# V rows of one token tile gathered token by token and summed on TensorE, and all gate matrices built before the last front

## The chip, the core and the metric

The kernel is one program on one core of a Trainium2 chip. The metric is the device time of one execution in microseconds. The core has TensorE (PE), VectorE (DVE), ScalarE (ACT), GpSimd (POOL) and SyncE (SP), each with its own queue of instructions that it takes in order, and 16 DMA engines that all queues share. TensorE runs at one of two clocks, 1.2 or 2.4 GHz; the profile gives the granted clock as a share of the higher one.

## The reference, cut to what matters

A sequence of 1024 tokens with 1024 features runs through one layer: a mixer (three recurrent branches, HGRN2, S5 and RG-LRU, between two projections) and a PEER layer with 16384 experts. Each expert is one row of `u_tab` and one row of `v_tab`. For each token, eight heads pick 16 experts each, so a token has 128 slots.

```python
x = x + gt1 * (y @ w_out[l])
h2 = rms_norm(x, g_ffn[l]) * (1.0 + sc2) + sh2
...
act = jax.nn.gelu(jnp.einsum('td,thkd->thk', hb, u_tab[eb]))
out = jnp.einsum('thk,thkd->td', gb * act, v_tab[eb])
x = x + gt2 * out          # then a final rms_norm
```

Everything is fp32.

## The kernel before

The 1024 tokens are eight tiles of 128. They go through the mixer in four fronts of two tiles each, F0 to F3; a front ends with the product keys (`product_keys`), which choose the experts of its two tiles. The recurrences make F0 to F3 follow one another.

The PEER layer is worked in two ways. Tiles 0, 1, 6 and 7 are gathered. In the U phase of a tile, slot k gathers for each of the 128 tokens the row of its k-th expert from `u_tab` (an indirect DMA on GpSimd's queue, 128 rows of 4 KB, into a buffer `row`), and VectorE multiplies it with the token's features and sums (L929). The V phase gathers from `v_tab`, again tokens on partitions, and VectorE adds weight times row to `fin` (L944). There are four buffers `row` in the fronts and a fifth in the dense stage.

Tiles 2 to 5 (`DSET`) are dense: every expert is computed for all of their 512 tokens, and the result is weighted with a gate matrix that is zero where a token did not choose the expert. `gates` builds these matrices: for each quad of four tokens it makes one-hot rows of the two halves of the expert number (`oh`), multiplies them on TensorE (`gk`), copies to `stg`, and stores 16 tokens at a time to `gd` in DRAM. There are 32 quads in a tile. `dense` then streams both tables through TensorE: transposes, products A with the features, gelu, the gates, products V.

The order is set in two steps. `PLAN` lists the steps: `("F", b)` is a front, `("P", u, v)` gathers the U slots of tile u and the V slots of tile v, `("G", n)` builds n gate matrices, `("D",)` is the dense stage, `("R",)` adds the fifth row buffer, `("E",)` ends. From that a planner with its own cost model arranges each engine's queue ahead of time by priority. Steps P carry a handicap of `PRI` = 3000 places, so they fill gaps. Work that comes later in the list may start earlier when its inputs and a free buffer are there. `dense` closes the pools of the fronts and puts its own tiles in their place, so it starts only when the fronts, their routing and all gate matrices are done; the row buffers stay.

The list before reads: F0, P(0, -), F1, F2, two gate matrices, P(-, 0), P(1, -), F3, two gate matrices, dense, R, P(-, 1), P(6, -), P(7, 6), P(-, 7), E.

Of the kernel before, what the change touches and what calls it, by code (L numbers as in the profile page):

```python
# [10 lines left out]
F32 = mybir.dt.float32  # L11
I32 = mybir.dt.int32
# [28 lines left out]
RTG = ()  # L41
RTS = ()
OHB = 1
GPRI = [0, 0, 0, 0]
SCP = 3
RSB = 2
PRI = 3000
# [16 lines left out]
PAD = 320  # L64
HRN = 2
EB = 3
PLAN = [("F", 0), ("P", 0, None), ("F", 1), ("F", 2), ("G", 2), ("P", None, 0), ("P", 1, None), ("F", 3), ("G", 2), ("D",), ("R",), ("P", None, 1), ("P", 6, None), ("P", 7, 6), ("P", None, 7), ("E",)]
NH = 4
HP = 8
TOPK = 16  # L70
# [17 lines left out]
def trunk(ctx, tc, x, c, w_mod, b_mod, g_mix, w_in, hgrn_lb_logits, s5_a_re, s5_a_im, s5_b_re, s5_b_im,  # L88
# [56 lines left out]
    V.memset(ones, 1.0)  # L145
    epsc = keep.tile([128, 1], F32, name="epsc")
    V.memset(epsc, EPS)
    one = keep.tile([128, 1], F32, name="one")
    V.memset(one, 1.0)

    iof = keep.tile([128, 128], F32, name="iof")
    G.iota(iof, [[1, 128]], base=0, channel_multiplier=0, allow_small_or_imprecise_dtypes=True)
# [194 lines left out]
    def front(t0, NT):  # L347
# [27 lines left out]
        def s5_parts():  # L375
# [23 lines left out]
            V.tensor_tensor(w[:, :, :, 0], w[:, :, :, 0], x_[:, :, :, 0], OP.add)  # L399
            yield  # L400
            for ri in range(2):
                if n == dec.shape[-1]:
                    wf = w[:, ri].rearrange("p k n -> p (k n)")
                    V.tensor_tensor_scan(wf, dec.rearrange("p k n -> p (k n)"), wf, 0.0, OP.mult, OP.add)
                else:
                    for k in range(8):
                        V.tensor_tensor_scan(w[:, ri, k], dec[:, k, 0:n], w[:, ri, k], 0.0, OP.mult, OP.add)

            xs = T4().rearrange("p (r k n) -> p r k n", r=2, k=8)[:, :, :, 0:n]
            V.tensor_copy(xs[:, :, :, 0], s5s)  # L410
# [329 lines left out]
    def route(r, eid, j):  # L740
        dense = j is not None
        best, ef = r
        if dense:
            sc4 = sm.tile([128, 2 * 8 * NCAND], F32, name="oh", bufs=OHB)
            tf = sc4[:, 0:2 * NS].rearrange("p (a s) -> p a s", a=2)
            ti = sc4[:, 2 * NS:4 * NS].bitcast(I32).rearrange("p (a s) -> p a s", a=2)
            eid = sc4[:, 4 * NS:5 * NS].bitcast(I32)
            V.tensor_copy(eid, ef.rearrange("p h k -> p (h k)"))
            gate = sc4[:, 5 * NS:6 * NS].rearrange("p (h k) -> p h k", h=HP)
        else:  # L750
            gate = pk_.tile([128, HP, TOPK], F32, name="gate", bufs=EB)
        V.tensor_tensor(gate, best, best[:, :, 0:1].to_broadcast([128, HP, TOPK]), OP.subtract)
        S.activation(gate, gate, AF.Exp)
        gs = sm.tile([128, HP], F32, name="gs")
        V.tensor_reduce(gs, gate, AX.X, OP.add)
        V.reciprocal(gs, gs)
        V.tensor_tensor(gate, gate, gs.unsqueeze(2).to_broadcast([128, HP, TOPK]), OP.mult)
        if not dense:
            return eid, gate

        V.tensor_single_scalar(ti[:, 0], eid, 7, OP.arith_shift_right)
        V.tensor_single_scalar(ti[:, 1], eid, 127, OP.bitwise_and)
        V.tensor_copy(tf, ti)
        bk = ph.tile([128, 512], F32, name="rt").rearrange("p (a s) -> p a s", a=4)
        P_.transpose(bk[:, 0], tf[:, 0], ident)
        P_.transpose(bk[:, 1], tf[:, 1], ident)
        P_.transpose(bk[:, 2], gate.rearrange("p h k -> p (h k)"), ident)
        tT = gp.tile([128, 3, NS], F32, name="tT", bufs=len(DSET))
        S.copy(tT, bk[:, 0:3])
        return tT, None  # L770
# [13 lines left out]
    def gates(j, tT):  # L784

        for c in range(128 // GT):
            stg = gp.tile([128, NK, GT], F32, name="stg", bufs=1)
            for q in range(GT // 4):
                pg = pg_.tile([128, 4, 128], F32, name="gk")
                oh = gp.tile([128, 2, 4, 128], F32, name="oh2", bufs=OB)  # L790

                for i in range(4):
                    t = c * GT + q * 4 + i
                    V.tensor_scalar(oh[:, 0, i], iof, tT[:, 0, t:t + 1], tT[:, 2, t:t + 1], op0=OP.is_equal, op1=OP.mult)
                    S.activation(oh[:, 1, i], iof, AF.Abs, bias=tT[:, 1, t:t + 1], scale=-1.0)
                S.activation(oh[:, 1], oh[:, 1], AF.Relu, bias=one, scale=-1.0)  # L796
                for i in range(4):
                    mm(pg[:, i], oh[:, 1, i], oh[:, 0, i], True, True)
                S.copy(stg[:, :, q * 4:q * 4 + 4].rearrange("p a t -> p t a"), pg)  # L799
            D.dma_start(out=gd[j * (128 // GT) + c], in_=stg)  # L800
# [136 lines left out]
    def v_slot(o, k):  # L937
# [5 lines left out]
        else:  # L943
            V.scalar_tensor_tensor(o.fin, vr, o.wgt[:, k:k + 1], o.fin, op0=OP.mult, op1=OP.add)  # L944

    def v_end(o):
        t, tmp = o.t, o.fin
        V.tensor_tensor(tmp, tmp, bcast["gt2"], OP.mult)
        finish(t, tmp, row)
# [46 lines left out]
    def slots(tu, tv):  # L996
# [11 lines left out]
        if v is not None:  # L1008
            v_end(v)

    head = front(*blocks[0])
    ahead = [head]
    next(head)
# [218 lines left out]
    for k in range(8):  # L1232
        V.scalar_tensor_tensor(toep[:, k], ident, dcol[:, k:k + 1], toep[:, k], op0=OP.mult, op1=OP.add)


    NST = TBM // T4S
    dec = const.tile([128, 8, NST], F32, name="dec")
    V.tensor_copy(dec, mT.unsqueeze(2).to_broadcast([128, 8, NST]))
    V.memset(dec[:, :, 0:1], 0.0)
    tau = CS()[:, 0:NST]  # L1240
    G.iota(tau, [[1, NST]], base=1, channel_multiplier=0, allow_small_or_imprecise_dtypes=True)
    rotc = const.tile([128, 8, NST], F32, name="rotc")
# [24 lines left out]
    for step in PLAN:  # L1267
# [9 lines left out]
        elif step[0] == "D":  # L1277
            dense()
        elif step[0] == "R":
            rows_.extend(more)  # L1280
        elif step[0] == "E":
            dense_end()
        else:
            phase(step[1], step[2])
# [31 lines left out]
```

## Time and profile before

| | us |
|---|---|
| median of 3 runs | 3267.55 (3264.48 to 3271.3) |
| the profiled execution | 3274.55 |
| its span, first to last instruction | 3272.8 |

| engine | busy, us | share of the span |
|---|---|---|
| PE (matmul) | 2853.3 | 87% |
| DVE | 2654.4 | 81% |
| POOL | 1305.0 | 40% |
| ACT | 1121.9 | 34% |

Busy time is the union of an engine's instructions. Matmuls are pipelined, so the mean duration of one is longer than its share of the busy time. An fp32 matmul leaves two records. A wait is put down to the instruction that released it.

### The profile page before, as it was taken

The numbers are of one execution on the slowest core, as the hardware profiler recorded it, in microseconds if no ns is written. First come the engines' busy times: TensorE is split into PE (matmuls) and PEld (weight loads), VectorE is DVE, ScalarE is ACT, GpSimd is POOL, SyncE is SP. The second block draws the span as 40 slices with busy tenths as digits, with TensorE's granted clock in tenths as the row PEclk, the third lists the DMA queues.
The fourth block names the chain that finished last, engine by engine and source line by source line (L and its number), as shares of the span: only waits on it lengthen the run. The fifth ranks groups of instructions, "written<-read, shape, count | busy, mean of one in ns | idle before, by whom it ended". The sixth has DMA issues, their size and how long they took to land.

```text
span 3272.8 us, 46195 instructions
## 1 busy us (share of the span) xinstructions
PE 2853.3 (87%) x16525; PEld 2439.7 (75%) x16525; DVE 2654.4 (81%) x5925; ACT 1121.9 (34%) x2123; POOL 1305.0 (40%) x1155
## 2 busy tenths in 40 slices
PE   5998975788778985678679999999999999999997
PEld 3765855476676865557569888988988988988886
DVE  6241898689987999768869889988999999899845
ACT  3212321123387651575822222222222222222222
POOL 0000146534444346430235545555555555455301
PEclk8998986899679985778589999999999999999998
DMA  5353687999689986894399989999999999899822
GB/s 153 115 155 122 183 293 242 324 340 303 210 286 350 310 283 222 285 325 140 134 319 338 326 307 336 348 345 345 338 344 349 343 352 347 311 330 341 297 91 78
DMA packets 490373, 896.77 MB, mean 274 GB/s; under 512 B 29608, under 2 KB 306720, under 8 KB 486048
## 3 DMA queue, kind: packets, MB, share of 16 engines
q0 software_dynamic: 147456, 536.94, 46.1%
q1 hardware_dynamic: 333312, 342.92, 32.0%
q10 hardware_dynamic: 9376, 13.96, 1.3%
q8 instruction: 131, 2.15, 0.3%
q14 instruction: 98, 0.80, 0.1%
HBM read 847.57 MB, written 46.14 MB: 273 GB/s over the span
## 4 chain that ended last, share of the span: by engine, by line
PE 41%; DVE 20%; DMA 16%; issue 11%; ACT 6%; POOL 5%; ACTq 0%; SPq 0%; POOLq 0%; DVEq 0%
PE A L139 13%; PE V L139 12%; PE bank L139 8%; DMA row<-in_peer_u_dram,eid 5%; DVE row L929 4%; PE wq L139 4%; POOL row L923 4%; DVE fin L944 3%; DMA row<-in_peer_v_dram,eid 3%; PE gk L139 2%; PE T L844 2%; DMA gd<-stg 2%; ACT stg L799 1%; POOL row L939 1%; DMA vn<-in_peer_v_dram 1%
## 5 line engine op out<-in xcount | busy, mean ns | idle before, releaser
L939 POOL DMA_INDIRECT row<-in_peer_v_dram,eid x512 | 622.2, 1215 | 691.2 <-DVE fin L944 360.4
L923 POOL DMA_INDIRECT row<-in_peer_u_dram,eid x512 | 638.2, 1246 | 622.9 <-DVE row L929 282.1
L139 PE MATMUL V<-vh,w 128*128 128x256 f32 x4096 | 768.6, 283 | 11.3 <-ACT vh L869 4.7
L929 DVE SCALAR_TENSOR_TENSOR row<-row,h 128x1024 f32<-128x1024 f32 x512 | 619.1, 1219 | 95.6 <-DMA row<-in_peer_u_dram,eid 92.0
L944 DVE SCALAR_TENSOR_TENSOR fin<-row,wgt,fin 128x1024 f32<-128x1024 f32 x508 | 649.4, 1278 | 50.0 <-DMA row<-in_peer_v_dram,eid 45.0
L139 PEld LDWEIGHTS V<-vh,w 128*128 128x128 f32 x4096 | 644.8, 189 | 22.2 <-ACT w L858 5.4
L139 PE MATMUL V<-vl,w 128*128 128x256 f32 x2048 | 562.1, 281 | 8.5 <-DVE vl L871 8.4
L139 PE MATMUL A<-hh,ul 128*128 128x512 f32 x1024 | 408.9, 399 | 14.6 <-DVE ul L846 14.6
L139 PE MATMUL A<-hh,uh 128*128 128x512 f32 x1024 | 416.6, 407 | 0.4 <-ACT uh L845 0.3
L139 PE MATMUL A<-hl,uh 128*128 128x512 f32 x1024 | 404.7, 395 | 0.0
L139 PEld LDWEIGHTS V<-vl,w 128*128 128x128 f32 x2048 | 389.0, 190 | 14.0 <-DVE vl L871 10.4
L869 ACT CAST vh<-vn 128x1024 fp32r<-128x1024 f32 x128 | 134.7, 1052 | 457.0 <-PE V L139 385.0
L139 PE MATMUL bank<-hT,w 128*128 128x256 f32 x1152 | 271.5, 392 | 20.8 <-DMA w<-in_w_in_dram 11.6
L139 PE MATMUL gk<-oh 128*128 128x128 f32 x1024 | 195.5, 352 | 95.8 <-ACT oh L796 56.3
L139 PEld LDWEIGHTS gk<-oh 128*128 128x128 f32 x1024 | 176.8, 255 | 117.9 <-ACT oh L796 81.4
L139 PEld LDWEIGHTS bank<-hT,w 128*128 128x128 f32 x1152 | 221.4, 197 | 56.6 <-issue 10.9
L139 PE MATMUL wq<-hT,w 128*128 128x256 f32 x1024 | 238.9, 388 | 5.1 <-DMA w<-in_peer_w_q_dram 5.1
L845 ACT CAST uh<-T 128x512 fp32r<-128x512 f32 x256 | 147.4, 586 | 273.7 <-PE T L844 267.9
L139 PEld LDWEIGHTS A<-hh,ul 128*128 128x128 f32 x1024 | 195.1, 191 | 54.8 <-DVE ul L846 21.1
L139 PEld LDWEIGHTS A<-hl,uh 128*128 128x128 f32 x1024 | 194.7, 190 | 37.1
L139 PEld LDWEIGHTS A<-hh,uh 128*128 128x128 f32 x1024 | 195.1, 190 | 34.8 <-ACT uh L845 1.3
L139 PEld LDWEIGHTS wq<-hT,w 128*128 128x128 f32 x1024 | 194.9, 195 | 31.2 <-issue 5.2
(422 smaller groups left out, 4084.6 us busy)
## 6 DMA issues: line engine op xcount, KB each, us to landing
vn<-in_peer_v_dram SPq DMA_DIRECT2D x128, 512.0 KB
un<-in_peer_u_dram SPq DMA_DIRECT2D x128, 512.0 KB
w<-in_w_in_dram SPq DMA_DIRECT2D x88, 512.0 KB
w<-in_peer_w_q_dram SPq DMA_DIRECT2D x64, 512.0 KB
gd<-stg SPq DMA_DIRECT2D x32, 1024.0 KB
gt<-gd SPq DMA_DIRECT2D x16, 2048.0 KB
w<-in_w_mod_dram SPq DMA_DIRECT2D x48, 512.0 KB
w<-in_w_out_dram SPq DMA_DIRECT2D x32, 512.0 KB
```

The lines of the kernel that those rows point to most:

```text
L139: P_.matmul(o, l, r, start=st, stop=sp)
L799: S.copy(stg[:, :, q * 4:q * 4 + 4].rearrange("p a t -> p t a"), pg)
L844: P_.transpose(bk[:, k], un[:, kk * 128:kk * 128 + 128], ident)
L845: S.copy(uh, bk)
L869: S.copy(vh, vn)
L923: G.indirect_dma_start(out=ur, out_offset=None, in_=u_tab, in_offset=bass.IndirectOffsetOnAxis(ap=o.eid[:, k:k + 1], axis=0))
L929: V.scalar_tensor_tensor(ur, ur, 1.0, o.h2, op0=OP.mult, op1=OP.mult, accum_out=o.act[:, k:k + 1])
L939: G.indirect_dma_start(out=vr, out_offset=None, in_=v_tab, in_offset=bass.IndirectOffsetOnAxis(ap=o.eid[:, k:k + 1], axis=0))
L944: V.scalar_tensor_tensor(o.fin, vr, o.wgt[:, k:k + 1], o.fin, op0=OP.mult, op1=OP.add)
```

## The change

The V phase of tile 0 is done by a new step M (`v_matmul`). It transposes expert numbers and weights of the tile, so that the 128 slots of a token lie on partitions. For each half of the 1024 features and each i from 0 to 31 it gathers the half rows (2 KB each) of the experts of four tokens, i, 32 + i, 64 + i and 96 + i: four gathers into two `row` buffers. Each token's 128 half rows are then multiplied by its weights on TensorE. The stationary operand is a slice of 32 columns of `zq`, zero but for one column that ScalarE fills with the weights of that token, and the result adds into one of four strips of 32 partitions of a PSUM bank. After 32 steps VectorE multiplies the bank by `gt2`.

Further parts: all four gate matrices stand ahead of F3 in the list, the last two with a handicap of 500 and 900 places (`GPRI`); in `gates` VectorE makes both one-hots with one comparison and ScalarE scales one of them by the gate, in place of Abs and Relu; the transposes of the gate rows move from the bank `rt` to `gk`, and M's sum takes that bank; the S5 scan runs over 64 elements at a time and its table `dec` goes.

```diff
-GPRI = [0, 0, 0, 0]
+GPRI = [0, 0, 500, 900]
...
-PLAN = [("F", 0), ("P", 0, None), ("F", 1), ("F", 2), ("G", 2), ("P", None, 0), ("P", 1, None), ("F", 3), ("G", 2), ("D",), ("R",), ("P", None, 1), ("P", 6, None), ("P", 7, 6), ("P", None, 7), ("E",)]
+PLAN = [("F", 0), ("P", 0, None), ("F", 1), ("F", 2), ("G", 4), ("M", 0), ("P", 1, None), ("F", 3), ("D",), ("R",), ("P", None, 1), ("P", 6, None), ("P", 7, 6), ("P", None, 7), ("E",)]
...
             for ri in range(2):
-                if n == dec.shape[-1]:
-                    wf = w[:, ri].rearrange("p k n -> p (k n)")
-                    V.tensor_tensor_scan(wf, dec.rearrange("p k n -> p (k n)"), wf, 0.0, OP.mult, OP.add)
...
+                for k in range(8):
+                    V.tensor_tensor_scan(w[:, ri, k], mT[:, k:k + 1].to_broadcast([128, n]), w[:, ri, k], 0.0,
+                                         OP.mult, OP.add)
...
-        bk = ph.tile([128, 512], F32, name="rt").rearrange("p (a s) -> p a s", a=4)
+        bk = pg_.tile([128, 4, 128], F32, name="gk")
...
+                t4 = slice(c * GT + q * 4, c * GT + q * 4 + 4)
+                V.tensor_tensor(oh, iof.unsqueeze(1).unsqueeze(1).to_broadcast([128, 2, 4, 128]),
+                                tT[:, 0:2, t4].unsqueeze(3).to_broadcast([128, 2, 4, 128]), OP.is_equal)
                 for i in range(4):
                     t = c * GT + q * 4 + i
-                    V.tensor_scalar(oh[:, 0, i], iof, tT[:, 0, t:t + 1], tT[:, 2, t:t + 1], op0=OP.is_equal, op1=OP.mult)
-                    S.activation(oh[:, 1, i], iof, AF.Abs, bias=tT[:, 1, t:t + 1], scale=-1.0)
-                S.activation(oh[:, 1], oh[:, 1], AF.Relu, bias=one, scale=-1.0)
+                    S.activation(oh[:, 0, i], oh[:, 0, i], AF.Copy, scale=tT[:, 2, t:t + 1])
...
+    def v_matmul(o):
+
+        v_start(o)
+        et = gp.tile([128, 2, 4, 128], F32, name="oh2", bufs=OB)[:, 0, 0:2]
+        V.tensor_copy(et[:, 0], o.eid)
+        bk = pg_.tile([128, 4, 128], F32, name="gk")
+        P_.transpose(bk[:, 0], et[:, 0], ident)
+        P_.transpose(bk[:, 1], o.wgt, ident)
+        wT = gp.tile([128, 4, 32], F32, name="wT")
+        S.copy(wT.rearrange("p g i -> p (g i)"), bk[:, 1])
+        e2 = gp.tile([128, 2, 128], I32, name="e2")
+        for h in range(2):
+            V.tensor_scalar(et[:, h], bk[:, 0], 2.0, float(h), op0=OP.mult, op1=OP.add)
+        V.tensor_copy(e2, et)
+        halves = v_tab.rearrange("e (h d) -> (e h) d", h=2)
+        for h in range(2):
+            pv = ph.tile([128, 512], F32, name="va")
+            for i in range(32):
+                z = zq[:, i % 2]
+                S.copy(z[:, :, 31], wT[:, :, i])
+                for g0 in (0, 2):
+                    vr = row().rearrange("p (g d) -> p g d", g=2)
+                    for g in range(2):
+                        t = 32 * (g0 + g) + i
+                        G.indirect_dma_start(out=vr[:, g], out_offset=None, in_=halves,
+                                             in_offset=bass.IndirectOffsetOnAxis(ap=e2[:, h, t:t + 1], axis=0))
+                    for g in range(2):
+                        gs = slice(32 * (g0 + g), 32 * (g0 + g) + 32)
+                        mm(pv[gs], z[:, g0 + g, 31 - i:63 - i], vr[:, g], i == 0, i == 31)
+            hs = slice(h * 512, h * 512 + 512)
+            V.tensor_tensor(o.fin[:, hs], pv, bcast["gt2"][:, hs], OP.mult)
+        finish(o.t, o.fin, row)
...
+    zq = const.tile([128, 2, 4, 63], F32, name="zq")
+    G.memset(zq, 0.0)
...
-    dec = const.tile([128, 8, NST], F32, name="dec")
-    V.tensor_copy(dec, mT.unsqueeze(2).to_broadcast([128, 8, NST]))
-    V.memset(dec[:, :, 0:1], 0.0)
...
+        elif step[0] == "M":
+            at = tc.cur_priority
+            tc.cur_priority = at + PRI
+            v_matmul(toks[step[1]])
+            tc.cur_priority -= PRI
```

## Rows read from the trace of the kernel before

**Rows 1.** Stages: us, busy us of PE, PEld, DVE, ACT, POOL; clock, DMA share, GB/s.

```profile
697.00:1085.00 388.00, 326.62 (x1671) 269.62 (x1670) 351.14 (x965) 206.46 (x456) 161.50 (x155) 0.86 0.87 292
1085.00:1240.00 155.00, 130.91 (x716) 109.99 (x714) 150.66 (x576) 80.74 (x164) 64.14 (x64) 0.90 0.86 285
1240.00:1460.00 220.00, 152.34 (x711) 123.32 (x712) 176.44 (x407) 99.34 (x211) 106.85 (x94) 0.73 0.82 284
1460.00:1530.00 70.00, 61.43 (x331) 55.30 (x329) 57.36 (x351) 35.10 (x84) 2.20 (x12) 0.95 0.52 166
1530.00:1650.00 120.00, 66.68 (x272) 58.21 (x272) 103.14 (x353) 94.82 (x204) 23.67 (x30) 0.55 0.43 157
1650.00:3110.00 1460.00, 1423.16 (x9324) 1282.80 (x9324) 1317.66 (x1761) 392.62 (x595) 763.25 (x617) 0.99 0.94 334
3110.00:3273.00 163.00, 138.31 (x919) 125.27 (x917) 79.62 (x117) 44.11 (x86) 11.32 (x8) 0.93 0.25 84
```

**Rows 2.** The chain by line, in 697 to 1085, then 1530 to 1650.

```profile
by line: DVE fin L944 10.4%; issue 10.4%; PE bank L139 8.0%; DMA row<-in_peer_v_dram,eid 7.1%; DMA w<-in_peer_w_q_dram 5.7%; PE wq L139 5.3%; PE gk L139 5.0%; ACT oh L795 4.4%; ACT stg L799 3.7%; DMA gd<-stg 3.2%; DVE ef L738 2.7%; DVE oh L
...
by line: DMA gd<-stg 29.7%; ACT stg L799 16.0%; issue 14.5%; PE gk L139 13.7%; ACT oh L795 11.4%; ACT oh L796 7.4%; DVE oh L794 1.7%; ACT L753 1.1%; DVE ef L738 0.7%; DVE oh L735 0.6%; DVE inds L687 0.5%; DVE rest L688 0.4%; SPq L835 0.4%; 
```

**Rows 3.** Tile row, 697 to 1085: ns min/median/max, first to last start, form.

```profile
L939 POOL DMA_INDIRECT row<-in_peer_v_dram,eid x128: 936/941/2994, 696.8 to 1076.6; - x128
L944 DVE SCALAR_TENSOR_TENSOR fin<-row,wgt,fin x127: 1224/1273/1286, 709.6 to 1084.0; 128x1024 f32<-128x1024 f32 x127
...
L942 DVE TENSOR_SCALAR fin<-row,wgt x1: 737/737/737, 707.7 to 707.7; 128x1024 f32<-128x1024 f32 x1
```

**Rows 4.** Groups on VectorE, whole span: busy us, mean ns, idle before.

```profile
L404 DVE TENSOR_TENSOR_SCAN s<-dec,s 128x512 f32<-128x512 f32 x8 | 9.3, 1201 | 0.0
...
L471 DVE TENSOR_TENSOR_SCAN lr<-lr,lru_h 128x256 f32<-128x256 f32 x8 | 5.5, 735 | 0.0
...
L948 DVE TENSOR_TENSOR fin<-fin,gt 128x1024 f32<-128x1024 f32 x4 | 4.9, 1218 | 0.0
```

**Rows 5.** Groups in 1530 to 1650 us: busy us, mean ns, idle before.

```profile
L794 DVE TENSOR_SCALAR oh<-iof,tT 128x128 f32<-128x128 f32 x136 | 38.3, 345 | 8.6 <-PE gk L139 8.4
L799 ACT COPY stg<-gk 128x512 f32<-128x512 f32 x34 | 34.2, 1030 | 10.8 <-DMA gd<-stg 7.1 <-PE gk L139 3.6
...
L944 DVE SCALAR_TENSOR_TENSOR fin<-row,wgt,fin 128x1024 f32<-128x1024 f32 x17 | 21.9, 1288 | 5.1 <-DMA row<-in_peer_v_dram,eid 4.9
```

**Rows 6.** Tile oh, whole span: ns min/median/max, first to last start.

```profile
L795 ACT ACTIVATE oh<-iof,tT x512: 378/390/508, 877.6 to 1636.1; 128x128 f32<-128x128 f32 x171
L794 DVE TENSOR_SCALAR oh<-iof,tT x512: 297/342/695, 878.0 to 1633.1; 128x128 f32<-128x128 f32 x171
L796 ACT ACTIVATE oh<-oh,one x128: 704/721/829, 881.6 to 1636.5; 128x512 f32<-128x512 f32 x128
...
L748 DVE CAST oh<-ef x4: 211/222/461, 867.9 to 1339.1; 128x128 int32<-128x128 f32 x4
```

**Rows 7.** Groups by form, PE, 0 to 1650: busy us, mean ns, idle before.

```profile
L139 PE MATMUL wq<-hT,w 128*128 128x256 f32 x1024 | 238.9, 388 | 5.1 <-DMA w<-in_peer_w_q_dram 5.1
...
L139 PE MATMUL bank<-w,hT 128*128 128x512 f32 x128 | 57.8, 596 | 0.0
```

**Rows 8.** Timeline of PE, 439.5 to 443.6: start us, us, what.

```profile
439.15 1.24 PE L139 MATMUL bank<-hT,w 128*128 128x256 f32 x5
440.33 2.06 PE L139 MATMUL bank<-u,ident 128*32 128x64 f32 x60
```

**Rows 9.** Tile stg, whole span: ns min/median/max, first to last start.

```profile
L800 SPq DMA_DIRECT2D gd<-stg x32: 319/338/902, 894.5 to 1640.5; - x32
```

**Rows 10.** Stages, instructions on tile gk alone: PE, PEld, DVE, ACT, clock.

```profile
1050.00:1150.00 100.00, 19.91 (x144) 19.20 (x144) 0.00 (x0) 18.74 (x18) 1.00 0.95 312
...
1530.00:1650.00 120.00, 66.68 (x272) 58.21 (x272) 0.00 (x0) 34.22 (x34) 0.55 0.43 157
```

**Rows 11.** Tile fin, whole span: ns min/median/max, first to last start.

```profile
L944 DVE SCALAR_TENSOR_TENSOR fin<-row,wgt,fin x508: 1224/1278/1350, 709.6 to 3094.3; 128x1024 f32<-128x1024 f32 x170
```

More of the change, by code (lines that the diff above doesn't have):

```diff
@@ L147, in trunk @@
     V.memset(epsc, EPS)
-    one = keep.tile([128, 1], F32, name="one")
-    V.memset(one, 1.0)
     iof = keep.tile([128, 128], F32, name="iof")
@@ L401, in s5_parts @@
             for ri in range(2):
-                if n == dec.shape[-1]:
-                    wf = w[:, ri].rearrange("p k n -> p (k n)")
-                    V.tensor_tensor_scan(wf, dec.rearrange("p k n -> p (k n)"), wf, 0.0, OP.mult, OP.add)
-                else:
-                    for k in range(8):
-                        V.tensor_tensor_scan(w[:, ri, k], dec[:, k, 0:n], w[:, ri, k], 0.0, OP.mult, OP.add)
+                for k in range(8):
+                    V.tensor_tensor_scan(w[:, ri, k], mT[:, k:k + 1].to_broadcast([128, n]), w[:, ri, k], 0.0,
+                                         OP.mult, OP.add)
             xs = T4().rearrange("p (r k n) -> p r k n", r=2, k=8)[:, :, :, 0:n]
```

## The prediction

> **What bounds the kernel now.** I read three views in this order: busy time by stage, the chain of waits inside the stages that the change touches, and the groups of instructions that it edits. The stages [rows 1] show two regimes. From 1650 us on (the dense experts) TensorE is busy for 1423 of 1460 us at a granted clock of 0.99: it is the bound, and nothing in the diff removes work from it. Before 1650 no engine is full. From 697 us, when the V slots of tile 0 begin, to 1650, VectorE is busy for 351.1 + 150.7 + 176.4 + 57.4 + 103.1 = 838.7 of 953 us (0.88). TensorE is busy for 738 us, but at clocks of 0.55 to 0.95. So the change can only move the start of the dense stage, at 1650 us. Two pieces stand ahead of it. In 697 to 1085 the chain [rows 2] goes through the V slots: 10.4% fin on VectorE and 7.1% V gathers, 17.5% of 388 us, 68 us. In 1530 to 1650 it consists of gate matrices: their store, their copy, their matmul and their two ScalarE steps make up over 70% of 120 us.
>
> **What the change removes.** The V phase of tile 0 leaves VectorE: 127 slots by 1.273 us, one of 0.74 us [rows 3] and the multiplication by gt2 (1.22 us) [rows 4], 163.6 us in all. Two multiplications of half the length from PSUM come back, at most 2.4 us. In gates, one comparison of 1024 elements takes the place of four fused ones. L948, an operation on 1024 elements, costs 1.22 us [rows 4]; the four cost 38.3/34 = 1.13 us [rows 5]. That is 0.09 us more for each of 128 quads, 11 us. A bound below is no change, one above the medians, 4 x 0.34 [rows 6], which would make it 19 us less. ScalarE loses Relu (0.72 us) and swaps four Abs for four scaled copies of the same size, taken at the same 0.39 us [rows 6]: with the copy to stg (1.03 us) [rows 5] a quad goes from 4 x 0.39 + 0.72 + 1.03 = 3.31 to 2.59 us. In the tail the 34 quads took 34 x 3.31 = 113 of 120 us: ScalarE paced it.
>
> **What it adds, small things.** The S5 scan goes from 2 x 512 elements to 16 x 64 per front. 512 elements cost 1.20 and 256 cost 0.735 us [rows 4]: 1.82 ns an element and 0.27 us fixed, so 64 elements cost 0.385 us. A front pays 16 x 0.385 - 2.4 = 3.8 us more, the two fronts after 697 us 7.5 us. The 64 copies into zq have four elements a partition: below an Abs (0.39 us) [rows 6], at most 25 us of ScalarE, which idles for 182 of 388 us there [rows 1]; without that cover they would lie on the path of the matmuls, at the same 25 us. GpSimd issues 256 gathers of half rows in place of 128. An issue takes 0.94 us at the median and 2.99 at most [rows 3], and nothing shows whether a half row is cheaper; I take the same. Two issues are then 1.9 us a row buffer, against a pace of 388/128 = 3.03 us now, so GpSimd has cover; at the bottom (half price) nothing changes, at 2 x 1.5 us it would just reach the old pace. The bytes are the same.
>
> **What it adds on TensorE.** There are 256 fp32 matmuls of 32 by 512. The product keys make 512 matmuls and show 1024 records, so a matmul is two records, and 512 columns cost 57.8/128 = 0.452 us a record [rows 7]. One after another that is 256 x 2 x 0.452 = 231 us, the upper bound. But the four groups write four different strips of 32 output partitions. The kernel has such matmuls already, the regrouping in S5: 60 records of 64 columns in 2.06 us, 34 ns each [rows 8], where one after another would be 0.452 x 64/512 = 56 ns. They overlap by 1.65, which makes 140 us here. If all four strips ran together it would be 58 us, the lower bound. I take a factor of 2, 116 us: short records carry more fixed time than those of 512 columns, but two gathers fill one buffer, so the strips become ready in pairs.
>
> The Trainium skill, "TensorEngine Tiling (Array Packing)", sections Theoretical Speedup and Key Properties, says two things of this: tiles of 32 columns can run up to four at once, and a change of the tiling mode drains the engine. By the first the price would be the 58 us above; the trace agrees that strips overlap, but only by 1.65. By the second every step between a front's matmul and these would lose time; in the one such step shown, the first narrow matmul starts at 440.33, ahead of the modelled end (439.15 + 1.24 us) of the wide ones [rows 8], so no loss can be read there.
>
> **Where the gates move.** Now tile 5's routing reaches its gate rows only at 1339 us [rows 6], and its gates stand behind the last front. With VectorE freed from 697 us on it should get there earlier, and all four gate matrices are ahead of F3, the last two with a handicap of 500 and 900 in priority. Each quad's instructions move: four ScalarE copies, four matmuls, the copy to stg, and on SP's queue 16 stores gd that now stand among the weight loads of F3, 0.34 us of issue each [rows 9] (5.4 us in all). What stays in the tail is F3's own routing: 103.1 - 38.3 (gates) - 21.9 (early V slots of tile 1) [rows 1, 5] = 43 us of VectorE. At 0.88 that is 49 us, so the tail can lose up to 71 us. The 34 quads then need 88 us of ScalarE in 1240 to 1530, which has 290 - 134 = 156 us idle.
>
> **The sum.** I work it as time from 697 us to the dense stage, by engine. VectorE: 838.7 - 163.6 + 2.4 + 11 + 7.5 - 21.9 (the slots of tile 1 only fill) = 674 us, at today's share of 0.88 766 us. TensorE: the gate matmuls cost 19.91/144 = 138 ns a record at clock 1.00 and 66.68/272 = 245 ns at 0.55 [rows 10], so work scales with the clock, and busy time times clock is the work at full clock: 281 + 118 + 111 + 58 + 37 = 605 us. With 116 it is 721 us. The best stage of the fronts, 1460 to 1530, gets 61.4/70 x 0.95 = 0.83 of full-clock time out of TensorE [rows 1]; at that share 721 us need 869 us. TensorE is the longer one, so it decides: dense starts at 697 + 869 = 1566 in place of 1650, 84 us earlier. Dense itself stays at 3273 - 1650 us. The profiled execution has a span of 3272.8 us and took 3274.55 us, 1.8 us around the span and 7.0 above the median of 3267.55 shown; I take 84 us off the median: **3184 us**.
>
> **Rivals.**
> Four strips together (chance 0.20): 605 + 58 = 663 us, at 0.83 799 us, near the 766 of VectorE. Dense starts 154 us earlier: 3114 us. For it speaks that the matmuls of one step stand next to each other on the queue; against it the 1.65 of [rows 8] and the pairs of gathers. This is what the rule of the tiling page named above would give.
>
> TensorE becomes the bound (0.12), the case on the other side: the matmuls run one after another, because the strips wait for different gathers and each waits in TensorE's own queue. 605 + 231 = 836 us at 0.83 are 1007 us, dense starts 54 us later: 3322 us. The point at which this decides is 0.83 x 953 - 605 = 186 us of added TensorE time; below it the kernel gets faster. Against it speaks the overlap shown.
>
> The new phase is slow and the U slots of tile 1 fall into the dense stage (0.06). They wait for the same four row buffers. At 3.03 us a buffer the phase ends at 1085 as now. At 7 us it ends at 1593, dense can start only then (57 us early), and 128 slots come on top of it. The last slot now ends at 3094 [rows 11]; some 617 slots in 1444 us are 2.34 us each, and the 179 us behind them hold 76 more; the other 52 cost 122 us: 3267.55 - 57 + 122 = 3333 us. Up to 5.5 us a buffer nothing is lost. In front of a late gather everything on TensorE's queue would wait, and ScalarE behind it, which waits for results.
>
> The gates of tiles 4 and 5 finish last all the same (0.09), since their handicap puts them behind much of F3: of the 84 us most of the 71 in the tail are lost, leaving some 15 to 40: about 3240 us. No change that can be told (0.05): slots were filler on VectorE, and what they freed is taken up by waits for TensorE.
>
> **Chances and range.** The forecast itself, 40 to 130 us faster, has 0.48. Faster by over 0.2% (6.5 us, about what a measurement can tell): 0.48 + 0.20 + 0.09 = 0.77; within it 0.05; slower 0.18. The likeliest case alone runs from 3138 to 3228. The range goes from 3095, somewhat beyond the four strips, to 3290, which leaves out most of the two slower cases (0.18) and little below.
>
> **What would show it.** The first load of the dense stage's U tables (un) and its first transposes at about 1566 us; VectorE from 697 us to there near 674 us busy, TensorE near 0.9 of the time at clocks above 0.9; the new matmuls at 0.2 to 0.3 us a record in sum (116 us over 512 records is 0.23 us); 0.94 us a half gather; the last gd store ahead of the end of F3's routing; the dense stage of 1623 us unchanged. I am wrong if the new matmuls cover more than 186 us, if U gathers of tile 1 run after the dense stage has begun by more than 76 slots, or if dense takes longer than 1640 us.

## The result, and the profile after

The changed kernel took 3672.3 us (median of 4 runs, 3668.4 to 3680.8) against 3266.0 us for the kernel before on the same chip: 1.1247 times as long (95% interval 1.122 to 1.1275). The forecast of 3184 us had the wrong sign, and its range ended at 3290. The profiled execution has a span of 3668.1 us, 395 more than before.

Stages of the changed kernel (columns as in [rows 1]):

```profile
697.00:1099.00 402.00, 361.23 (x1760) 289.89 (x1760) 235.05 (x1090) 119.06 (x241) 10.34 (x50) 0.90 0.38 113
1099.00:1514.00 415.00, 339.91 (x1917) 295.51 (x1915) 282.13 (x740) 309.22 (x731) 7.58 (x25) 0.85 0.35 122
1514.00:1881.00 367.00, 269.34 (x512) 36.79 (x512) 1.74 (x5) 12.70 (x66) 243.92 (x259) 0.89 0.66 196
1881.00:3500.00 1619.00, 1562.79 (x10190) 1405.22 (x10191) 1450.21 (x2044) 434.61 (x661) 845.14 (x691) 0.98 0.94 332
3500.00:3668.00 168.00, 9.53 (x52) 8.82 (x51) 129.24 (x142) 10.54 (x33) 111.89 (x84) 0.53 0.77 268
```

Read the POOL column first. It is nearly empty from 697 to 1514 us: no row is gathered for over 800 us (the gathers ahead of this end at 687 us, the next starts at 1513), where the kernel before gathered V rows of tile 0 and then U rows of tile 1 [rows 1, 3]. The fronts and gates end at 1514, earlier than the 1650 of before. Then comes a stage that the kernel before did not have: 367 us with nothing but the sum of tile 0, VectorE and ScalarE all but idle. Dense starts at 1881, 231 us late, and lasts 1619 us; the forecast was 1623. A last stage of 168 us, with TensorE all but idle, is new too. 231 and 168 us, less the 4 us by which dense was shorter, are the 395.

Tile `row` and tile `gk` of the changed kernel (ns min/median/max, first to last start). Here L918 and L924 are the U slots, L934 and L939 the V slots, L965 the new gathers, L760 the routing's transposes, L794 the copy of the gates:

```profile
L918 POOL DMA_INDIRECT row<-in_peer_u_dram,eid x512: 935/942/2013, 387.5 to 3363.4; - x171
...
L139 PE MATMUL va<-row,zq x512: 589/617/1063, 1521.4 to 1880.1; 128*32 128x512 f32 x171
...
L939 DVE SCALAR_TENSOR_TENSOR fin<-row,wgt,fin x381: 1270/1280/2303, 2221.5 to 3649.0; 128x1024 f32<-128x1024 f32 x191
...
L965 POOL DMA_INDIRECT row<-in_peer_v_dram,e x256: 943/949/958, 1515.4 to 1874.3; - x128
```
```profile
L139 PE MATMUL gk<-oh x1024: 272/275/583, 1098.1 to 1512.8; 128*128 128x128 f32 x171
...
L794 ACT COPY stg<-gk x128: 988/1039/1132, 1099.3 to 1513.1; 128x512 f32<-128x512 f32 x128
...
L760 PE MATMUL gk<-ident,oh x4: 272/272/273, 780.8 to 1097.9; 128*128 128x128 f32 x4
```

Two starts are to be seen. The gates begin at 1098.1 us, right behind the last of the four routings (1097.9), though the first routing was done at 781; before, they began at 878 [rows 6]. And the sum's first gather is issued at 1515.4, right behind the last copy of the gates (1513.1). The timeline shows the second hand-over:

```profile
1511.79 1.02 ACT L794 COPY stg<-gk 128x512 f32<-128x512 f32 x1 [1.31 <-PE gk L139]
1511.85 0.23 DVE L945 CAST oh<-eid 128x128 f32<-128x128 int32 x1 [4.43 <-PE gk L139]
...
1512.94 0.27 PE L947 MATMUL gk<-ident,oh 128*128 128x128 f32 x1
...
1514.81 0.29 DVE L954 CAST e<-oh 128x256 int32<-128x256 f32 x1
1515.38 0.95 POOL L965 DMA_INDIRECT row<-in_peer_v_dram,e  x1 [1.14 <-DVE e L954]
```

L945 is the first instruction of the sum. It only copies expert numbers known since the first front (the U slots of tile 0 gather by them from 387.5 us on), but it writes `oh` (in the program `oh2`), the tile that the gates' one-hots use, and it was released by a gate matmul. Groups and waits in the stage of the sum (1514 to 1881 us):

```profile
L139 PE MATMUL va<-row,zq 128*32 128x512 f32 x512 | 269.3, 683 | 98.0 <-DMA row<-in_peer_v_dram,e 64.4 <-issue 16.9 <-ACT zq L960 11.7
...
L960 ACT COPY zq<-wT 128x4 f32<-128x4 f32 x64 | 12.4, 198 | 343.0 <-PE va L139 195.5 <-issue 89.5 <-remote 58.0
```
```profile
PEld va L139 <- DMA row<-in_peer_v_dram,e: 208.8, 172, 4.6
ACT zq L960 <- PE va L139: 195.5, 33, 11.8
```

A matmul of the sum covers 269.3/256 = 1.05 us, and most wait for a gather of their own. The U slots of tile 1, which use the same buffers and stand behind the sum, go into the dense stage with all V slots of tiles 1, 6 and 7; the last V slot comes at 3649 us instead of 3094 [rows 11].

### The profile page after: what moved, and what is told of

Read it like the earlier page. It is cut to its first block, busy times and chain, and to the rows that moved or that the text cites. A ratio compares the mean times of both kernels' runs of the same rounds, so it can differ in the third digit from the quotient of the medians.

```text
span 3668.1 us, 46842 instructions
## 1 busy us (share of the span) xinstructions
PE 3100.3 (85%) x17039; PEld 2454.2 (67%) x17039; DVE 2524.2 (69%) x5471; ACT 1056.7 (29%) x2058; POOL 1384.5 (38%) x1284
## 4 chain that ended last, share of the span: by engine, by line
PE 36%; DVE 18%; issue 16%; POOL 12%; DMA 11%; ACT 5%; SPq 1%; POOLq 0%; ACTq 0%; another core or an unknown queue 0%; DVEq 0%
PE bank L139 12%; PE A L139 7%; PE V L139 7%; POOL row L918 5%; PE wq L139 4%; POOL row L934 4%; DMA row<-in_peer_v_dram,eid 4%; POOL row L965 3%; DVE row L924 3%; DMA row<-in_peer_v_dram,e 3%; PE gk L139 2%; DMA row<-in_peer_u_dram,eid 2%; DVE fin L939 2%; DVE oh L787 1%; PE T L839 1%
## 5 line engine op out<-in xcount | busy, mean ns | idle before, releaser
L918 POOL DMA_INDIRECT row<-in_peer_u_dram,eid x512 | 614.7, 1201 | 612.1 <-DVE row L924 351.7
L924 DVE SCALAR_TENSOR_TENSOR row<-row,h 128x1024 f32<-128x1024 f32 x512 | 620.8, 1220 | 102.7 <-DMA row<-in_peer_u_dram,eid 100.0
L934 POOL DMA_INDIRECT row<-in_peer_v_dram,eid x384 | 483.9, 1260 | 448.4 <-DVE fin L939 167.9
L939 DVE SCALAR_TENSOR_TENSOR fin<-row,wgt,fin 128x1024 f32<-128x1024 f32 x381 | 491.8, 1291 | 54.0 <-DMA row<-in_peer_v_dram,eid 52.0
L139 PE MATMUL va<-row,zq 128*32 128x512 f32 x512 | 269.3, 683 | 98.0 <-DMA row<-in_peer_v_dram,e 64.4
L710 POOL COPY cid<-cidx 128x32 f32<-128x32 f32 (+2 forms) x96 | 22.3, 268 | 710.3 <-DVE cidx L701 709.6
L965 POOL DMA_INDIRECT row<-in_peer_v_dram,e x256 | 242.7, 948 | 118.3 <-issue 67.1
L139 PEld LDWEIGHTS va<-row,zq 128*32 128x32 f32 x512 | 36.8, 114 | 329.9 <-DMA row<-in_peer_v_dram,e 208.8
L139 PE MATMUL gk<-oh 128*128 128x128 f32 x1024 | 181.4, 335 | 62.5 <-ACT stg L794 31.4
```

What stands on the lines that cost most here:

```text
L139: P_.matmul(o, l, r, start=st, stop=sp)
L710: G.tensor_copy(cid8[:, :, o:o + n], cidx[:, :, p0:p0 + (n - 1) * d + 1:d])
L918: G.indirect_dma_start(out=ur, out_offset=None, in_=u_tab, in_offset=bass.IndirectOffsetOnAxis(ap=o.eid[:, k:k + 1], axis=0))
L924: V.scalar_tensor_tensor(ur, ur, 1.0, o.h2, op0=OP.mult, op1=OP.mult, accum_out=o.act[:, k:k + 1])
L934: G.indirect_dma_start(out=vr, out_offset=None, in_=v_tab, in_offset=bass.IndirectOffsetOnAxis(ap=o.eid[:, k:k + 1], axis=0))
L965: G.indirect_dma_start(out=vr[:, g], out_offset=None, in_=halves, in_offset=bass.IndirectOffsetOnAxis(ap=e2[:, h, t:t + 1], axis=0))
```

## The experiments

Theory A: tiles with one name hand out their buffers in the order of the list. The change put the sum's first tiles under the names `oh2` and `gk`, behind all gates, and the routing's transposes under `gk`, ahead of them. Rival B: the new matmuls cost their time wherever they stand. Rival C: the other edits cost it. All ratios are to the kernel before on the same chip, with 95% intervals; differences in microseconds are between runs on several chips, on which the kernel before took 3262 to 3269 us. Of the line `PLAN` only the steps that differ are shown.

**own_tiles**, the change with tiles of its own for the sum:

```diff
-        et = gp.tile([128, 2, 4, 128], F32, name="oh2", bufs=OB)[:, 0, 0:2]
+        e2 = gp.tile([128, 2, 128], I32, name="e2")
+        et = e2.bitcast(F32)
...
-        bk = pg_.tile([128, 4, 128], F32, name="gk")
+        bk = ph.tile([128, 512], F32, name="va").rearrange("p (a s) -> p a s", a=4)
```

> The change with one difference: the two tiles that the sum of tile 0 shared with the gates (the SBUF tile with the name oh2 and the PSUM tile with the name gk) are tiles of its own. Theory A (a shared tile is handed out in the order of the list, so the sum of tile 0 stood behind all gates of tiles 2 to 5, began at 1512 us, and the U slots of tile 1 and all that follows moved with it): the first gather of the sum now comes near 700 us, its 256 gathers run beside the fronts, the U slots of tile 1 come ahead of the dense stage, and the time falls from 3672 to between 3230 and 3400 us. Theory B (the 256 matmuls, each of which waits for its own gather in TensorE's queue, cost their 270 to 370 us wherever they stand): the fronts grow by what the sum no longer takes behind them, and the time stays above 3580 us. Theory C (the other edits of the change, those of the gates and the scan, make up the loss): no change, 3640 to 3700 us.

3334.4 us, 1.0198 (1.0164 to 1.0231): 338 us back. The first gather moves from 1515 to 706.5 us. The gates still begin behind the last routing (L760's last at 1180.3):

```profile
L965 POOL DMA_INDIRECT row<-in_peer_v_dram,e x256: 943/949/2201, 706.5 to 1247.4; - x128
```
```profile
L794 ACT COPY stg<-gk x128: 1002/1046/1124, 1182.3 to 1702.4; 128x512 f32<-128x512 f32 x128
```

**m_first**, the change with M ahead of G in the list:

```diff
-("F", 2), ("G", 4), ("M", 0),
+("F", 2), ("M", 0), ("G", 4),
```

> The change with the sum of tile 0 ahead of the gates in the list; it still shares both tiles with them. Theory A: the sum waits for one routing of tiles 2 to 5 at most, begins between 700 and 1100 us, and the gates and the U slots of tile 1 stand behind it; the time falls to between 3250 and 3450 us. Theory B: above 3580 us, since the matmuls that wait for gathers are only moved ahead. Theory C: 3640 to 3700 us.

3438.8 us, 1.0525 (1.049 to 1.0561). The first gather is at 1114.2, after the last routing (1097.7), for which `gk` still makes the sum wait. More than half of the loss (233 of 406 us) goes by list order alone; rival B's 3580 is missed.

**no_m**, the change with V slots for tile 0:

```diff
-("G", 4), ("M", 0),
+("G", 4), ("P", None, 0),
```

> The change with tile 0's V rows taken in slots on VectorE, as in the kernel before; the gates' new form, their place ahead of the last front and the scan in pieces stay. Theory A: the gates still end near 1500 us, the slots of tile 0 and tile 1 run beside the fronts as before, and the time is 3190 to 3290 us, near the kernel before (3266) or under it. Theory B says the same of this kernel. Theory C: above 3400 us.

3376.7 us, 1.034 (1.0306 to 1.0374). Outside A's range, and below C's: without any sum the change is still 107 us slow. The tile `gk` shows where; the gates wait for the last routing again, which now comes later, beside the V slots on VectorE:

```profile
L794 ACT COPY stg<-gk x128: 989/1042/1112, 1307.7 to 1730.7; 128x512 f32<-128x512 f32 x128
...
L760 PE MATMUL gk<-ident,oh x4: 273/374/477, 874.4 to 1305.2; 128*128 128x128 f32 x4
```

**no_m_rt**, the same with the routing off the gates' tile:

```diff
-        bk = pg_.tile([128, 4, 128], F32, name="gk")
+        bk = ph.tile([128, 512], F32, name="va").rearrange("p (a s) -> p a s", a=4)
         P_.transpose(bk[:, 0], tf[:, 0], ident)
```

> The last kernel without the matmul sum (V rows of tile 0 in slots on VectorE; 3377 us), with one difference: the routing's transposes are put into a PSUM tile of their own (va) and no longer into the gates' (gk). Theory D (in the changed kernel the gates of tiles 2 and 3 stand behind the routing of tile 5, for that tile alone: the first gate came at 1305 us there, at 882 us before): the gates begin near 900 us and end by about 1600 us where they ended at 1730; the dense stage begins 100 to 160 us earlier; 3200 to 3290 us. Rival E (the gates are late because VectorE, which also has tile 0's V slots, gets to the routing and the gates late, or because the gates' new form is slower): the gates still end after 1690 us, 3330 to 3390 us.

3211.2 us, 0.9847 (0.9823 to 0.9872): 166 us by that one name, and faster than both kernels. The gates begin at 890, not 1308:

```profile
L794 ACT COPY stg<-gk x128: 998/1047/1165, 890.0 to 1580.8; 128x512 f32<-128x512 f32 x128
```

Theory D holds. The other three edits, each alone in the kernel before, were run beside it.

**b_g4** (`PLAN` and `GPRI` alone):

```diff
-("F", 2), ("G", 2), ("P", None, 0), ("P", 1, None), ("F", 3), ("G", 2), ("D",),
+("F", 2), ("G", 4), ("P", None, 0), ("P", 1, None), ("F", 3), ("D",),
```

> The kernel before with the order of the list alone changed: all gates ahead of the V slots of tile 0 and of the last front, with the two priorities that the change gives them. Gates, scan, routing tile and V slots are as before. If the order helps: the 34 quads of gates that were left behind the fronts (1530 to 1650 us) move beside them, and the dense stage begins up to 100 us earlier: 3165 to 3250 us. If VectorE and ScalarE are full there and something else falls behind in exchange: 3250 to 3290 us. Rival E of the run above holds if it is slower than 3300 us.

3217.4 us, 0.987 (0.9846 to 0.9895).

**b_gates** (the gates' new form alone):

```diff
+                V.tensor_tensor(oh, iof.unsqueeze(1).unsqueeze(1).to_broadcast([128, 2, 4, 128]),
+                                tT[:, 0:2, t4].unsqueeze(3).to_broadcast([128, 2, 4, 128]), OP.is_equal)
...
-                    V.tensor_scalar(oh[:, 0, i], iof, tT[:, 0, t:t + 1], tT[:, 2, t:t + 1], op0=OP.is_equal, op1=OP.mult)
-                    S.activation(oh[:, 1, i], iof, AF.Abs, bias=tT[:, 1, t:t + 1], scale=-1.0)
-                S.activation(oh[:, 1], oh[:, 1], AF.Relu, bias=one, scale=-1.0)
+                    S.activation(oh[:, 0, i], oh[:, 0, i], AF.Copy, scale=tT[:, 2, t:t + 1])
```

> The kernel before with the gates' new form alone (one comparison of 128x1024 on VectorE, four scalings on ScalarE). From rows of both traces a quad costs VectorE 1.22 us in place of 4 x 0.354 = 1.42, ScalarE 4 x 0.394 + 1.04 = 2.62 in place of 3.34; but ScalarE's scalings now wait for VectorE's comparison, where both ran side by side. If ScalarE sets the 34 quads behind the fronts (3.5 us each), 34 x 0.7 = 24 us are gained: 3235 to 3260 us. If the longer chain sets them: 3260 to 3300 us.

3215.3 us, 0.9857 (0.9833 to 0.988): 47 us, more than the 24 expected for ScalarE's part of the 34 quads behind the fronts. Fewer quads are left there: 24 are copied after 1530 us, and 20 in b_g4, against 34 before.

**b_scan** (the scan alone):

```diff
+                for k in range(8):
+                    V.tensor_tensor_scan(w[:, ri, k], mT[:, k:k + 1].to_broadcast([128, n]), w[:, ri, k], 0.0,
```

> The kernel before with the scan in 8 pieces of 64 columns alone. VectorE has 64 x 0.27 = 17 us of scans less 12.5 measured in the changed kernel and 9.3 before, so 3 us more spread over three or four fronts: no measurable change, 3258 to 3280 us. If a scan in pieces costs more in the fronts' chains: up to 3300 us.

3262.6 us, 1.0006 (0.9989 to 1.0024): no change. Order and form each gain 45 to 47 us and together, with the scan, 51: they shorten the same tail of gates, whose last copy comes at 1591 us with the order, 1592 with the form and 1581 with both, against 1639 before.

**m_early**, own_tiles with the routing in `va` and M ahead of F2:

```diff
-("F", 1), ("F", 2), ("G", 4), ("M", 0),
+("F", 1), ("M", 0), ("F", 2), ("G", 4),
```

> The sum of tile 0 on tiles of its own and listed ahead of the third front, and the routing of tiles 2 to 5 off the gates' PSUM tile, so that both the sum and the gates can begin near 700 us. Theory A: the sum begins near 700 us, the gates too, both are done by 1450 us, and the time is 3150 to 3330 us, less than with either one alone late. Theory B: above 3580 us. In both, TensorE's own work ahead of the dense stage is the same 605 us at full clock plus 256 matmuls; with no overlap of strips (1.05 us each, 269 us) it ends near (605 + 269)/0.85 + 697 = 1725 us, 75 us later than before, which alone would give 3340 us.

3308.2 us, 1.0143 (1.0097 to 1.0188). Inside A's range, but only moved: `va` is now shared by the sum and the routing. The timeline shows the third routing's transposes behind the sum's last read:

```profile
1387.48 0.69 DVE L971 TENSOR_TENSOR fin<-va,gt 128x512 f32<-128x512 f32 x1 [23.99 <-PE va L139]
...
1388.23 0.33 PE L760 MATMUL va<-ident,oh 128*128 128x128 f32 x1 [0.16 <-DVE fin L971]
```

**no_share**, own_tiles in the change's own list order, with the routing in the fronts' PSUM tile:

```diff
-        bk = pg_.tile([128, 4, 128], F32, name="gk")
+        bk = pw.tile([128, 512], F32, name="wq").rearrange("p (a s) -> p a s", a=4)
```

> The change in its own list order, with nothing shared any more: the sum of tile 0 on tiles of its own, and the routing's transposes in a PSUM tile of the fronts (wq). If the two shared tiles explain all of the loss beyond the sum's own work: as m_early, 3280 to 3340 us (3308 there; the sum and the gates both begin between 700 and 900 us). If it is the place in the list that made m_early quicker than own_tiles: 3330 to 3400 us.

3251.7 us, 0.9949 (0.9929 to 0.9968): better than either case expected, 421 us under the change. `wq` and `va` are shared too, but not with the gates. The gates begin at 806 us and the gathers of the sum at 712; dense's first products come at 1498:

```profile
L794 ACT COPY stg<-gk x128: 994/1048/1194, 806.4 to 1461.6; 128x512 f32<-128x512 f32 x128
...
L965 POOL DMA_INDIRECT row<-in_peer_v_dram,e x256: 942/949/2407, 711.8 to 1354.8; - x128
```
```profile
L139 PE MATMUL A<-hh,uh x1024: 387/393/796, 1498.4 to 3195.9; 128*128 128x512 f32 x171
...
L139 PE MATMUL wq<-hT,w x1024: 377/379/795, 317.4 to 1553.0; 128*128 128x256 f32 x171
```

**rt_own**, the routing's transposes in `wq` alone, in the change:

> The change with the routing's transposes in the fronts' PSUM tile (wq) alone; the sum of tile 0 still shares its two tiles with the gates. The gates of tiles 2 and 3 begin near 880 us, those of 4 and 5 near 1100, and end near 1350; the sum still stands behind all of them (1350 to 1700 us), and the U slots of tile 1 behind the sum. Theory A: dense stage from about 1700 us, the slots late by some 300 us: 3430 to 3560 us. If the sum's late start were harmless once the gates are early: below 3350 us.

3513.2 us, 1.075 (1.0708 to 1.0792). The gates end at 1375, the sum runs from 1388 to 1739 us. So each name alone costs: the sum's 338 us (own_tiles) or 262 (with the routing apart, 3513 to 3252), the routing's 159 or 83 (3334 to 3252); together 421.

**no_share_strips**, four gathers ahead of four matmuls:

```diff
-                for g0 in (0, 2):
-                    vr = row().rearrange("p (g d) -> p g d", g=2)
+                vrs = [row().rearrange("p (g d) -> p g d", g=2) for _ in range(2)]
+                for g in range(4):
...
+                for g in range(4):
+                    gs = slice(32 * g, 32 * g + 32)
+                    mm(pv[gs], z[:, g, 31 - i:63 - i], vrs[g // 2][:, g % 2], i == 0, i == 31)
```

> As no_share, with four gathers ahead of four matmuls, one for each strip of 32 partitions, in place of two and two. In the trace of own_tiles four matmuls on four strips stood in 1.07 us once and in 3.21 us a moment later; the whole sum kept TensorE busy for 144 to 185 us of the runs with an early sum. Theory F (beside the late gates, what keeps these kernels above 3211 us is TensorE, whose busy share between 697 and 1262 us was 538 of 565): four together take 64 x 1.07 = 68 us, some 75 to 110 us less than in no_share, and the time falls by 50 to 110 us, to 3190 to 3270. Rival G (the gathers set the pace, 256 issues of 0.95 us on GpSimd's queue and the slots of tile 1 behind them): within 20 us of no_share.

3259.3 us, 0.9969 (0.9941 to 0.9997): no difference from no_share. This does not decide for G, because the edit did not reach the queue: the planner still puts the four matmuls in between others, mostly one or two at a time. TensorE's timeline of this run (xN counts records, two to a matmul):

```profile
887.01 1.05 PE L139 MATMUL va<-row,zq 128*32 128x512 f32 x2
...
888.63 1.05 PE L139 MATMUL va<-row,zq 128*32 128x512 f32 x4
...
909.55 1.07 PE L139 MATMUL va<-row,zq 128*32 128x512 f32 x8
```

One matmul takes 1.05 us, two take 1.05, four take 1.07: neighbours on different strips cost nothing more if their gathers have landed. Where they had not, four neighbours took three times as long (own_tiles; PEld are the weight loads):

```profile
905.48 3.21 PE L139 MATMUL va<-row,zq 128*32 128x512 f32 x8
...
906.45 0.14 PEld L139 LDWEIGHTS va<-row,zq 128*32 128x32 f32 x2 [0.83 <-DMA row<-in_peer_v_dram,e]
907.64 0.14 PEld L139 LDWEIGHTS va<-row,zq 128*32 128x32 f32 x2 [1.06 <-DMA row<-in_peer_v_dram,e]
```

**ns_knock**, no_share with 240 of 256 matmuls left out:

```diff
-                    for g in range(2):
+                    for g in range(2 if i in (0, 31) else 0):
                         gs = slice(32 * (g0 + g), 32 * (g0 + g) + 32)
```

> As no_share, with 240 of the 256 matmuls left out (the sum of tile 0 then has 8 of its 128 tokens, and the gathers, the weight copies, the buffers and all else stay). Theory F: TensorE is freed of some 140 to 170 us, and the time falls by 90 to 170 us, to 3140 to 3230. Rival G: within 20 us of no_share.

3207.2 us, 0.9824 (0.9789 to 0.9858): 45 us, half of the least that F expected. With neither V slots on VectorE nor the matmuls, it is no faster than no_m_rt, which has the slots (3211). TensorE's timeline shows a hole:

```profile
1182.08 0.33 PE L139 MATMUL bank<-s,toep 128*128 128x64 f32 x2
1257.85 0.48 PE L760 MATMUL wq<-ident,oh 128*128 128x128 f32 x1 [75.43 <-DVE oh L758]
```

and VectorE's groups name what it did meanwhile, from 1100 to 1265 us and in the hole alone (1182 to 1258 us):

```profile
L924 DVE SCALAR_TENSOR_TENSOR row<-row,h 128x1024 f32<-128x1024 f32 x68 | 82.5, 1217 | 15.1 <-DMA row<-in_peer_u_dram,eid 14.9
...
L924 DVE SCALAR_TENSOR_TENSOR row<-row,h 128x1024 f32<-128x1024 f32 x37 | 44.7, 1218 | 9.6 <-DMA row<-in_peer_u_dram,eid 9.6
```

The U slots of tile 1 took 44.7 of the 76 us, and waits for their gathers 9.6 more.

**ns_knock_p1** and **no_share_p1**, with the U slots of tile 1 behind F3 in the list:

```diff
-("P", 1, None), ("F", 3), ("D",),
+("F", 3), ("P", 1, None), ("D",),
```

> As ns_knock (240 of the 256 matmuls left out, so tile 0's sum has 8 of its 128 tokens), with the U slots of tile 1 listed behind the last front in place of ahead of it. Theory H (VectorE's freed time goes at once to these 128 slots of 1.22 us, 68 of them between 1100 and 1265 us, ahead of the routing of tiles 4 and 5, for which TensorE then stands 75 us): the hole closes, the fronts and gates end 60 to 110 us earlier, and the slots move into the end of the fronts and the dense stage; if the dense stage has room for them 3110 to 3180 us, if not 3190 to 3250. Rival J (the fronts are set by their own chain and by TensorE, 291 of 445 us at a clock of 0.79 there): the dense stage begins where it did (1566 us), 3195 to 3230 us.

> As no_share (all matmuls), with the U slots of tile 1 listed behind the last front. Theory H: TensorE was busy there for 0.93 of 697 to 1700 us and had no such hole, so the fronts gain at most 30 us and the slots end later than 3239 us: 3250 to 3330 us. Rival J: 3240 to 3265 us.

3213.4 us, 0.9831 (0.9782 to 0.9879), and 3251.6 us, 0.9954 (0.993 to 0.9979). Both lie in the ranges of rival J, and the first misses that of H, but this is inconclusive: the planner put the slots where they had been, and the hole stayed (72.17 us).

**ns_knock_u1** and **no_share_u1**, with 120 of these slots left out:

```diff
+        if o.t == 1 and k >= 8:
+            V.memset(o.act[:, k:k + 1], 0.0)
+            return
         ur = row()
```

> As ns_knock (240 of the 256 matmuls left out), and of the 128 U slots of tile 1 only 8 are done (the other 120 columns are set to zero), so neither tile 0's sum nor tile 1's is whole. Listing these slots later had not moved them (TensorE still stood 72 us for the routing), so now the work itself is out: 120 x 1.3 = 156 us of VectorE less. Theory H (these slots hold up the routing): the hole of 75 us in TensorE closes and the dense stage begins at 1460 to 1510 us in place of 1566. Rival J (TensorE and the fronts' own chain): the dense stage begins within 20 us of 1566. In both the time itself may fall by more, since the dense stage has 0 to 120 slots less to carry.

> As no_share (all matmuls), with the same 120 U slots of tile 1 left out. If TensorE is the bound with the matmuls in (0.93 busy from 697 to 1700 us), the fronts' last top-k (1744 us there) comes at most 30 us earlier and the dense stage's last matmul, at 3196 us, at most 30 us. If VectorE is still the bound: both 80 us earlier or more.

3085.7 us, 0.9427 (0.9396 to 0.9459): the hole is gone (the longest wait of TensorE's matmuls between 1085 and 1530 us is 4.9 us), and dense's first product starts at 1433.2, 132 us earlier than in ns_knock, more than theory H expected, while rival J expected less than 20. The left-out slots take their gathers with them, so VectorE's own time and its waits for these gathers are not told apart.

```profile
L139 PE MATMUL A<-hh,uh x1024: 387/392/628, 1564.9 to 3156.2; 128*128 128x512 f32 x171
...
L139 PE MATMUL A<-hh,uh x1024: 387/393/632, 1433.2 to 3036.3; 128*128 128x512 f32 x171
```

The second kernel took 3134.2 us, 0.9582 (0.955 to 0.9614): the last top-k of the fronts comes at 1600 instead of 1744 us, dense's last A product at 3086 instead of 3196. My expectation for the case that TensorE is the bound fell: with the matmuls in, the slots still hold up the end of the fronts.

## Why the prediction was wrong

**The step that failed** stands ahead of its sum: that the new phase begins at 697 us where the V slots did, and that with VectorE freed the gates get there earlier. The inputs were there: the cast of tile 5's routing came at 1091 us instead of 1339 [rows 6]. The buffers were not. Three lines of the diff name an existing tile (`oh2`, `gk` twice). Buffers of one name go round in list order, so the gates waited for the routing of tile 5, the sum for the last gate, and the U slots of tile 1 for the sum: the gates began at 1098 us, the sum at 1515, dense at 1881 in place of 1566. I costed the transposes themselves at nothing and never asked behind whom their tiles stand. With these three uses off the gates' names (no_share) the kernel took 421 us less, more than the 406 us lost.

**The rival that came nearest** was that the U slots of tile 1 fall into the dense stage (0.06, 3333 us). That happened and gave the stage of 168 us at the end. But it was put on a slow phase, 7 us a buffer; the phase ran at 367/128 = 2.87 us, faster than the 3.03 assumed. It came late. In no_share, mixed among the fronts, the same phase ran at 643/128 = 5.0 us a buffer, and the U slots of tile 1 behind it ran from 1377 to 1737 us, where the kernel before had them from 1093 to 1449: there the phase was slow, though under the 5.5 us up to which I expected no loss.

**TensorE's term** was 116 us, between 58 and 231. In the stage alone it was 269 us, above the upper bound: a matmul that stands alone covers 1.05 us (in no_share its two records start 0.45 us apart and the second lasts 0.59 to its modelled end), not the 2 x 0.452 of matmuls in a row [rows 7]. In no_share, mixed among the fronts, it was 153.4 us, 37 more than taken; there taking 240 matmuls out gave 45 us. The strips do overlap, fully, where the matmuls are neighbours on the queue and their gathers have landed: 1.07 us for four matmuls against 1.05 for one. The Trainium skill, "TensorEngine Tiling (Array Packing)", section Theoretical Speedup, gives up to four times for 32 columns; the trace agrees there. One of the two conditions was missing in each kernel: alone, each matmul waited for its own gather, and these are issued 1.25 us apart at the median; mixed, the planner split the four.

**The share of 0.83**, which turned TensorE's work into time, came from one stage and was too low. From 697 to 1498 us in no_share TensorE was busy for 752.4 of 801 us at a clock of 0.96, which is 0.90 of full-clock time.

**Dense starts 84 us earlier.** In no_share dense's first products came at 1498 us, earlier still than the 1566 forecast. Yet the time fell by only 0.5%. Dense did not wait for the last front and its routing to end, as I had assumed and as the section on the kernel before says: the remaining key products (until 1553 us) and top-k (until 1744) ran beside it. Its stage shows VectorE full and TensorE at 182 of 245 us (no_share, 1500 to 1745 us); 112 of VectorE's 235 us there are U slots of tile 1, and the length of dense was not the unchanged 1623 us:

```profile
1500.00:1745.00 245.00, 181.77 (x1010) 155.89 (x1009) 235.26 (x698) 48.37 (x82) 128.51 (x119) 0.87 0.89 295
```

Stages of one length that only shift were the wrong picture.

**VectorE's 164 us of V slots** left it as worked out: over the whole span it was busy 2654 us before and 2519 in no_share, 136 less, where the terms of the sum make 143. They gained little: in ns_knock the freed time went to U slots of tile 1, ahead of the routing for which TensorE stood. An engine's share of busy time did not tell which of its work others wait for. With those slots out the hole closed. Why no_share is faster than m_early by 57 us, where the sum and the routing share `va`, is read from the timeline and was not tried apart.

**ScalarE in the tail** was misread. 34 x 3.31 = 113 of 120 us adds up durations, and ScalarE's instructions overlap: its busy time in that stage is 94.8 us [rows 1], 0.79 of it, so that it paced the tail is not shown. That the new form gained 47 us there stands by its run alone.

**What held.** By durations a gate quad is 4 x 0.394 + 1.04 = 2.62 us of ScalarE (forecast 2.59), and VectorE's comparison 1.22; a half-row gather is issued in 0.949 us, like a whole one; the 64 copies into `zq` took 12.4 of at most 25 us; the scan keeps VectorE busy for 12.4 us in four fronts against 9.3 [rows 4], less than the 3.8 us a front forecast, and costs nothing in time. The tail of gates that could be lost (up to 71 us) gave 45 us by the order alone and 51 with the form. Dense lasted 1619 us in the changed kernel.

## What to carry to other kernels

When an edit takes a buffer under an existing name, list who else uses that name, in the order in which the program asks for it, and price a wait for the last one ahead; this was worth more than every instruction that was added or removed. When work leaves a busy engine, ask what takes the freed time first, and whether somebody waits for the work behind it. The parts of a change are worth running apart: here two of them gain 1.3 and 1.4% each, and with the routing on a tile of its own and V slots kept, the rest of the change runs in 3211 us, 1.5% under the kernel before.

## What was not expected of the hardware

Strips of 32 columns cost the same singly or four at a time: 1.05, 1.05 and 1.07 us for one, two and four fp32 matmuls of 512 columns that follow one another on TensorE's queue and have their operands, where the regrouping in S5 had shown an overlap of 1.65 [rows 8]. And an indirect gather of 128 rows of 2 KB takes GpSimd as long to issue as one of 4 KB, 0.949 against 0.942 us at the median.
